# First stretch: v gathered on scaled tokens, k on tokens shifted in place, and the shift's part of v summed on VectorE

## The chip, the cores and the metric

The kernel runs on one core of one Trainium2 chip. The metric is the device time of one execution in microseconds (us). The core has TensorE (PE in the profile; PEld is its weight load), VectorE (DVE), ScalarE (ACT) and GpSimd (POOL), and SyncE (SP), whose queue issues nearly all loads; most stores to DRAM are issued from POOL's queue. A matmul accumulates in PSUM tiles; ScalarE or VectorE copies them out.

## The reference, cut to what matters

One inference step over 640 tokens (512 latent ones, 128 of context) and two layers. Both layers begin with a modulated norm; layer 0 is attention:

```python
sh, sc, ga = adaln(cond, w_mod[l], b_mod[l])     # silu(cond) @ w_mod + b_mod, in three
h = rms_norm(y, g_pre[l]) * (1.0 + sc) + sh       # 640 x 2048
q, k, v, g = split(h @ w_in_attn)                 # 2048, 512, 512 and 2048 columns
q = rms_norm(q, q_norm); k = rms_norm(k, k_norm)  # per head of 128, then rotary positions
o = blocked_attention(q, k, v)
y = y + ga * rms_norm((o * silu(g)) @ w_out, g_post[l])
```

Latent and context tokens have their own `cond`, hence their own shift and scale, one value per feature. Each product is made of three matmuls over operands split in a high and a low part (hi, lo; wh, wl). Layer 1 has a linear recurrence in place of attention; its code is the same in both kernels. k and v of the context tokens are also outputs (new_cache_k, new_cache_v).

## The kernel before, in words

The normalized tokens stand in five tiles `xn`, 128 tokens each. The first stretch (inside `tc.manual_schedule()`, so in the order written) goes over the 2048 features in eight passes of 256, and a ninth that only finishes. Pass n does this, with the pieces interleaved on TensorE:

- `gemv0` four times (kb = 0 to 3): 512 rows of w_mod, 256 columns of shift and 256 of scale in one tile `raw` of 1 MB, are multiplied with the conditions (`c32`, 32 columns of which two count). Four matmuls of 512 columns go to four groups of 32 rows of `pm`.
- `x_t`: eight transposes of token tiles; `row0` copies `pm` out, `cols0` turns the row into columns by eight small matmuls with `sel4`; three VectorE instructions then make scale and shift of this pass.
- `put`: hi = token x scale + shift on ScalarE, the same once more in full precision (`v`), lo = v - hi on VectorE; once for the latent and once for the context tokens, whose transposes come between.
- `load_wv`, `split_w`, `v_part`: 256 rows of v's weights are loaded and split, and one pass later, when hi and lo of these features stand, five token tiles are gathered into v: 30 matmuls of 128x512 per pass (2 feature blocks x 5 token tiles x 3). v's accumulators are three PSUM tiles `pg0` to `pg2`.

After it, v is copied out into two `qf` tiles (pool `pb`, two buffers for all uses of `qf`) and written to `v_s` and new_cache_v. Then come, by `gemm_nat`, one block of k and four blocks of q, each 240 matmuls over the finished hi and lo with weights loaded by 1-MB tiles and split into `wh`, `wl` (a ring of three). A block's three accumulators are `pd` tiles, of which there are four. `norm_rope` copies each accumulator to a `qf` tile, squares it into a `qs` tile (both on ScalarE), and makes norm and rotary positions on VectorE; POOL's queue writes the result to `k_s` or `q_s`. Eight blocks of g follow (`gemm_T`), and attention reads all from DRAM.

Beside the blocks runs a generator `gemv` (layer 1's modulation on VectorE, 32 steps of about four instructions of 128x1024). `background` is called once per 1-MB weight tile; it adds 32/36 to a credit and runs one step for each whole unit of it. Outside the manual stretch a scheduler sets the order on each engine; code that is written earlier has priority, and `split_w` above all.

Of the kernel before, what the change touches and what calls it, by code (L numbers as in the profile page):

```python
# [44 lines left out]
def hybrid_step(ctx: ExitStack, tc: tile.TileContext, i, o):  # L45
# [219 lines left out]

    def gemv0(fb, kb, pm):


        raw = rawp.tile([128, 2048], F32, name="raw", tag="raw")
        r4 = raw.rearrange("p (k a n) -> p k a n", k=4, a=2)  # L270
        for a in range(2):
            SY.dma_start(r4[:, :, a], i["w_mod"][0, kb * 512:kb * 512 + 512,
                                                 a * D + fb * 256:a * D + fb * 256 + 256]
                         .rearrange("(k p) n -> p k n", p=128))
        for j in range(4):
            PE.matmul(pm[32 * j:32 * j + 32], c32[:, kb * 4 + j], raw[:, j * 512:j * 512 + 512],  # L276
                      start=(kb == 0), stop=(kb == 3))

    def row0(pm):
        row = pa.tile([128, 512], F32, name="row", tag="row", bufs=1)  # L280
        S.copy(row, pm)
        return row

    def cols0(fb, pm, row):

        pc = pm[:, :8]
        for b in range(4):
            PE.matmul(pc[:, 2 * b:2 * b + 2], row[:, b * 128:b * 128 + 128], sel4, start=True, stop=True)
        kt = fb * 2
        tmp = small.tile([128, 2, 2, 2], F32, name="mt", tag="mt")  # L290
        bm = VA[:, 32:64].rearrange("p (a k) -> p a k", a=2)[:, :, kt:kt + 2]
        V.tensor_tensor(tmp, pc.rearrange("p (a f c) -> p a f c", a=2, f=2),
                        bm.unsqueeze(3).to_broadcast([128, 2, 2, 2]), op=add)
        V.scalar_tensor_tensor(scale[0][:, kt:kt + 2], tmp[:, 1], 1.0,
                               VA[:, kt:kt + 2].unsqueeze(2).to_broadcast([128, 2, 2]), op0=add, op1=mult)
        V.tensor_copy(shift[0][:, kt:kt + 2], tmp[:, 0])

    def put(k, c, src, t):
        sc, sh = scale[0][:, k, c:c + 1], shift[0][:, k, c:c + 1]
        n = t.stop - t.start  # L300
        v = pa.tile([128, NL], F32, name="v", tag="v", bufs=2)
# [9 lines left out]

    def load_wv(fb):
        w = pa.tile([128, 1024], F32, name="wv", tag="wv", bufs=2)
        SY.dma_start(w.rearrange("p (k n) -> p k n", k=2),
                     w_in[fb * 256:fb * 256 + 256, 2560:3072].rearrange("(k p) n -> p k n", p=128))
        return w

    def v_part(fb, k2, toks, w):

        k = fb * 2 + k2  # L320
        for m in toks:
            t = slice(TOFF[m], TOFF[m] + 128)
            b = slice(k2 * 512, k2 * 512 + 512)
            mm3(vacc[m // 2][:, m % 2], hi[:, k, t], lo[:, k, t], w[0][:, b], w[1][:, b], k == 0, k == KT - 1)

    VA = load_cols("VA", [fold2(i["g_pre"]), fold2(i["b_mod"])])
    with tc.manual_schedule():
        for m in range(5):
            SY.dma_start(xn[m], x_rows(m))
        for m in range(5):  # L330
            load_x(m)
        wv = None
        for n in range(9):
            now = n < 8
# [12 lines left out]
            if n:
                v_part(n - 1, 0, (4,), wv)
            if now:
                xt = [x_t(n * 2 + f) for f in range(2)]  # L350
                wn = split_w(wn)
                gemv0(n, 3, pm)
                row = row0(pm)
            if n:
                v_part(n - 1, 1, (0, 1), wv)
            if now:
                cols0(n, pm, row)
            if n:
                v_part(n - 1, 1, (2, 3, 4), wv)
            if now:  # L360
# [8 lines left out]
                wv = wn  # L369
    VB = load_cols("VB", [fold2(i["conv_w"][0]), fold(i["conv_b"][0])], 80)  # L370
# [50 lines left out]

    gv = gemv()
# [641 lines left out]
```

## Time and profile before

| what | value |
|---|---|
| time, median of 3 runs (lowest, highest) | 1950.09 us (1949.22, 1951.38) |
| the profiled execution | 1950.84 us, of which the span of the trace is 1949.1 us |
| PE busy | 1885.3 us, 97% of the span |
| PEld busy | 1675.4 us, 86% |
| DVE busy | 1324.5 us, 68% |
| ACT busy | 864.5 us, 44% |
| POOL busy | 136.2 us, 7% |
| read from and written to HBM | 273.03 MB, 29.43 MB |

Durations and starts come from the profiled execution, whose own time is the span and 1.7 us around it. It is 0.75 us above the median. A busy share is an average over stages with different limits; a line of the timeline gives the start, the duration, and in brackets the idle time before it and what released the instruction. A matmul's duration overlaps the next one's, so the cost of one is the difference of two starts. The DMA share is the mean over 16 engines and can pass 1.

### The profile page before, as it was taken

What the parts mean: (1) busy time and instruction counts of PE and PEld (TensorE: products, weight loads), DVE (VectorE), ACT (ScalarE), POOL (GpSimd) and SP (SyncE); (2) the same over time, 40 slices, a digit from 0 to 9 for tenths busy, and PEclk for the clock granted to TensorE, in tenths of its full rate; (3) what the DMA queues carried; (4) which work ended last, traced back from release to release, by engine and by line L of the source; (5) the groups of instructions that cost most, each with busy time, mean ns of one, the idle gap of its engine ahead of it and who ended that gap; (6) DMA issues with size and microseconds to landing.
All of it is one profiled execution on the core that took longest, in us unless ns stands there. A gap on an engine that the chain in (4) does not pass through costs nothing.

```text
span 1949.1 us, 26788 instructions
## 1 busy us (share of the span) xinstructions
PE 1885.3 (97%) x10857; PEld 1675.4 (86%) x10857; DVE 1324.5 (68%) x1856; ACT 864.5 (44%) x1256; POOL 136.2 (7%) x218
## 2 busy tenths in 40 slices
PE   4999999999999899999999999899999999999997
PEld 1567887879999899998888889899999999988886
DVE  3237859758365389998857775875775674798646
ACT  4441223222221288882223555666466456652222
POOL 0000000000000001110000000110110010020000
PEclk9999999999999999999999999999999999999999
DMA  9995435536454212225545674323322322537446
GB/s 341 348 321 195 162 123 184 178 119 198 157 175 150 86 38 74 74 74 198 180 155 187 234 260 130 122 72 96 120 95 92 101 79 86 175 110 253 146 136 220
DMA packets 195900, 304.20 MB, mean 156 GB/s; under 512 B 7344, under 2 KB 124720, under 8 KB 193856
## 3 DMA queue, kind: packets, MB, share of 16 engines
q1 hardware_dynamic: 188944, 274.10, 42.5%
q0 software_dynamic: 6832, 28.38, 4.0%
q8 instruction: 85, 1.39, 0.3%
q14 instruction: 39, 0.32, 0.0%
HBM read 273.03 MB, written 29.43 MB: 155 GB/s over the span
## 4 chain that ended last, share of the span: by engine, by line
PE 83%; DVE 6%; ACT 5%; issue 2%; DMA 2%; SPq 1%; POOL 0%; DVEq 0%; ACTq 0%; POOLq 0%
PE pd L184 22%; PE pd L185 22%; PE pd L186 22%; PE pd L215 2%; PE pd L217 2%; PE pd L218 2%; PE pm L276 2%; PE ph L631 1%; PE pg L184 1%; ACT L938 1%; PE pg L185 1%; PE pg L186 1%; PE sp L184 1%; PE sp L185 1%; PE sp L186 1%
## 5 line engine op out<-in xcount | busy, mean ns | idle before, releaser
L179 ACT CAST wh<-raw 128x1024 fp32r<-128x1024 f32 x248 | 258.1, 1048 | 606.1 <-PE pd L186 331.6
L180 DVE TENSOR_TENSOR wl<-raw,wh 128x1024 fp32r<-128x1024 f32 x248 | 301.6, 1222 | 238.9 <-ACT wh L179 238.1
L184 PE MATMUL pd<-wh,hi 128*128 128x512 f32 x1040 | 411.2, 396 | 3.6 <-ACT qf L498 2.5
L185 PE MATMUL pd<-wl,hi 128*128 128x512 f32 x1040 | 410.6, 395 | 0.0
L186 PE MATMUL pd<-wh,lo 128*128 128x512 f32 x1040 | 410.3, 394 | 0.0
L184 PE MATMUL pd<-hi,wh 128*128 128x322 f32 x1280 | 399.2, 312 | 0.0
L186 PE MATMUL pd<-hi,wl 128*128 128x322 f32 x1280 | 397.0, 310 | 1.1 <-DVE wl L180 1.1
L185 PE MATMUL pd<-lo,wh 128*128 128x322 f32 x1280 | 397.5, 311 | 0.0
L186 PEld LDWEIGHTS pd<-hi,wl 128*128 128x128 f32 x1280 | 241.5, 189 | 1.6 <-DVE wl L180 1.6
L185 PEld LDWEIGHTS pd<-lo,wh 128*128 128x128 f32 x1280 | 242.2, 189 | 0.1
L184 PEld LDWEIGHTS pd<-hi,wh 128*128 128x128 f32 x1280 | 241.4, 189 | 0.5 <-ACT wh L179 0.3
L184 PEld LDWEIGHTS pd<-wh,hi 128*128 128x128 f32 x1040 | 195.8, 188 | 50.7 <-ACT qf L498 2.9
L186 PEld LDWEIGHTS pd<-wh,lo 128*128 128x128 f32 x1040 | 195.9, 188 | 46.1
L185 PEld LDWEIGHTS pd<-wl,hi 128*128 128x128 f32 x1040 | 195.9, 188 | 45.5 <-DVE wl L180 0.3
L741 DVE SCALAR_TENSOR_TENSOR ga<-raw,cT,ga 128x512 f32<-128x512 f32 x256 | 175.8, 748 | 15.7 <-DMA ga<-b_mod 13.0
L395 DVE SCALAR_TENSOR_TENSOR ga<-raw,cT,ga 128x1024 f32<-128x1024 f32 x120 | 149.8, 1279 | 27.4 <-DMA raw<-w_mod 26.8
L184 PE MATMUL pd<-xh,wh 128*128 128x322 f32 x256 | 81.5, 320 | 5.2 <-ACT xh L876 4.4
L215 PE MATMUL pd<-hi,wh 128*128 128x256 f32 (+1 forms) x256 | 80.7, 315 | 6.0 <-ACT wh L179 4.3
L218 PE MATMUL pd<-hi,wl 128*128 128x256 f32 (+1 forms) x256 | 80.2, 313 | 0.0
L217 PE MATMUL pd<-lo,wh 128*128 128x256 f32 (+1 forms) x256 | 80.1, 313 | 0.0
L185 PE MATMUL pd<-xl,wh 128*128 128x322 f32 x256 | 80.1, 314 | 0.0
L186 PE MATMUL pd<-xh,wl 128*128 128x322 f32 x256 | 79.9, 313 | 0.0
(238 smaller groups left out, 2813.6 us busy)
## 6 DMA issues: line engine op xcount, KB each, us to landing
raw<-w_mod SPq DMA_DIRECT2D x64, 1024.0 KB
raw<-w_in_lru SPq DMA_DIRECT2D x40, 1024.0 KB
raw<-w_in_attn SPq DMA_DIRECT2D x36, 1024.0 KB
raw<-w_mod SPq DMA_DIRECT2D x64, 512.0 KB
raw<-w_out_attn SPq DMA_DIRECT2D x20, 1024.0 KB
raw<-w_out_lru SPq DMA_DIRECT2D x20, 1024.0 KB
g_s<-qf POOLq DMA_DIRECT2D x16, 322.0 KB, 3.4
raw<-g_s SPq DMA_DIRECT2D x16, 322.0 KB
```

The costliest lines, as they stand in the source:

```text
L179: S.copy(wh, src)
L180: V.tensor_tensor(wl, src, wh.bitcast(F32), op=sub)
L184: PE.matmul(out, ah, bh, start=first, stop=False)
L185: PE.matmul(out, ah, bl, start=False, stop=False)
L186: PE.matmul(out, al, bh, start=False, stop=last)
L215: PE.matmul(outs[f], wh[:, c], hi[:, k, t], start=(k == 0 and first[f]), stop=False, skip_group_check=True)
L217: PE.matmul(outs[f], wh[:, c], lo[:, k, t], start=False, stop=False, skip_group_check=True)
L218: PE.matmul(outs[f], wl[:, c], hi[:, k, t], start=False, stop=(k == KT - 1), skip_group_check=True)
L276: PE.matmul(pm[32 * j:32 * j + 32], c32[:, kb * 4 + j], raw[:, j * 512:j * 512 + 512], start=(kb == 0), stop=(kb == 3))
L395: V.scalar_tensor_tensor(acc[c], w2[:, k2], cT[:, k, c:c + 1], acc[c], op0=mult, op1=add)
L631: PE.transpose(pt[:, c * 128:c * 128 + 128], P[:, b, c * 128:c * 128 + 128], ident)
L741: V.scalar_tensor_tensor(acc[:, c], raw[:, k4 * 512:k4 * 512 + 512], cT[:, kb * 4 + k4, c:c + 1], acc[:, c], op0=mult, op1=add)
```

## The change: what it does

The first stretch now has 17 passes. Passes 0 to 7 read only the scale half of w_mod. One `raw` tile holds 1024 rows of 256 columns, for two `gemv0`, each of four matmuls of 256 columns. `put` makes hi and lo from the token times the scale alone (lo by one VectorE instruction), and v is gathered on these. Passes 8 to 15 read the shift half, and `add_shift` adds the shift to hi and lo in place: u = hi + lo, hi = u + shift, lo = u + shift - hi. Behind it, in passes 9 to 16, k is gathered on the finished tokens in the way v was. v and k are copied into `xn` tiles, which are free by then, and written to the scratch arrays `v_r` and `k_r`. The `gemm_nat` block of k is gone; `norm_rope` loads k from `k_r`.

What v lacks is shift @ w_v, one row of 512 for each condition. The generator `v_shift` makes it first thing in the background: it loads v's weights again (four tiles of 1 MB), sums shift x weight over the 16 feature blocks on VectorE (32 instructions of 128x512, two conditions), splits the sum, adds over the partitions by four matmuls with `ones` into a `pd` tile, loads v back from `v_r` into `qf` tiles, adds, and writes v_s and new_cache_v. Then it goes on with `gemv`. The credit per call is 40/32.

```diff
+    def gemv0(part, fb, kb, pm):
+        if kb % 2 == 0:
+            raw = rawp.tile([128, 2048], F32, name="raw", tag="raw")
+            SY.dma_start(raw.rearrange("p (k n) -> p k n", k=8),
+                         i["w_mod"][0, kb * 512:kb * 512 + 1024, part * D + fb * 256:part * D + fb * 256 + 256]
                          .rearrange("(k p) n -> p k n", p=128))
+            rawg[0] = raw
         for j in range(4):
-            PE.matmul(pm[32 * j:32 * j + 32], c32[:, kb * 4 + j], raw[:, j * 512:j * 512 + 512],
+            n = ((kb % 2) * 4 + j) * 256
+            PE.matmul(pm[32 * j:32 * j + 32, :256], c32[:, kb * 4 + j], rawg[0][:, n:n + 256],
                       start=(kb == 0), stop=(kb == 3))
...
-        S.activation(hi[:, k, t], src, AF.Identity, scale=sc, bias=sh)
-        S.activation(v[:, :n], src, AF.Identity, scale=sc, bias=sh)
-        V.tensor_tensor(lo[:, k, t], v[:, :n], hi[:, k, t].bitcast(F32), op=sub)
+        S.activation(hi[:, k, t], src, AF.Identity, scale=sc)
+        V.scalar_tensor_tensor(lo[:, k, t], src, sc, hi[:, k, t].bitcast(F32), op0=mult, op1=sub)
+
+    def add_shift(k):
+        u = pa.tile([128, TE], F32, name="u", tag="u", bufs=2)
+        V.tensor_tensor(u, hi[:, k, :TE].bitcast(F32), lo[:, k, :TE].bitcast(F32), op=add)
+        for c, t in ((0, slice(0, NL)), (1, slice(PO, TE))):
+            sh = shift[0][:, k, c:c + 1]
+            S.activation(hi[:, k, t], u[:, t], AF.Identity, bias=sh)
+            V.scalar_tensor_tensor(lo[:, k, t], u[:, t], sh, hi[:, k, t].bitcast(F32), op0=add, op1=sub)
...
+    def evac(acc, dst):
+        for j, (a, ms) in enumerate(zip(acc, PAIRS)):
+            n = len(ms)
+            f = xn[j][:, :n * 512].rearrange("p (m n) -> p m n", n=512)
+            (V.tensor_copy if j == 1 else S.copy)(f, a)
+            G.dma_start(dst[ms[0] * 128:ms[0] * 128 + n * 128].rearrange("(m p) n -> p m n", p=128), f)
...
-        for n in range(9):
-            now = n < 8
+        for n in range(17):
+            now = n < 16
+            part, fb, pb_ = int(n < 8), n % 8, (n - 1) % 8
...
+            elif now:
+                if n == 8:
+                    evac(acc, v_r)
+                    acc = accs()
+                for f in range(2):
+                    add_shift(fb * 2 + f)
+            else:
+                evac(acc, k_r)
...
+    def v_shift():
+        acc = pb.tile([128, 1024], F32, name="ga0", tag="ga0")
+        a2 = acc.rearrange("p (c n) -> p c n", c=2)
+        for kb in range(4):
+            w = load_w(w_in, kb * 512, 4, 2560, 512)
...
+                        V.scalar_tensor_tensor(a2[:, c], wk, sh, a2[:, c], op0=mult, op1=add)
+                if k4 % 2:
+                    yield
+        pg = psd()
+        ah, al = split_w(acc)
+        for c in range(2):
+            PE.matmul(pg[:, c], ones, ah[:, c * 512:c * 512 + 512], start=True, stop=False)
+            PE.matmul(pg[:, c], ones, al[:, c * 512:c * 512 + 512], start=False, stop=True)
+        for ms in PAIRS:
...
+            vf = pb.tile([128, 2, 512], F32, name="qf", tag="qf", bufs=2)
+            SY.dma_start(vf[:, :n], v_r[rows].rearrange("(m p) n -> p m n", p=128))
+            V.tensor_tensor(vf[:, :n], vf[:, :n], pg[:, ms[0] // 4].unsqueeze(1).to_broadcast([128, n, 512]), op=add)
+            G.dma_start(v_s[rows].rearrange("(m p) n -> p m n", p=128), vf[:, :n])
...
-        credit[0] += 32 / 36
+        credit[0] += 40 / 32
...
-    norm_rope(gemm_nat(w_in, 2048, background), "k", k_s, o["new_cache_k"])
+    norm_rope([None] * 3, "k", k_s, o["new_cache_k"])
```

How instructions move is shown at three places; a row gives the line, the operation, what it writes and reads, and its size, and the numbers behind names tell tiles of one name apart. The first is one pass on VectorE, before:

```order
L180 TENSOR_TENSOR wl_792<-wv_750,wh_791 128x1024
L292 TENSOR_TENSOR mt_814<-pm_742,VA_173 128x8
L294 SCALAR_TENSOR_TENSOR scale0_152<-mt_814,VA_173 128x4
L296 COPY shift0_150<-mt_814 128x4
L304 TENSOR_TENSOR lo_119<-v_827,hi_118 128x512
L304 TENSOR_TENSOR lo_119<-v_831,hi_118 128x512
L304 TENSOR_TENSOR lo_119<-v_838,hi_118 128x128
L304 TENSOR_TENSOR lo_119<-v_842,hi_118 128x128
```

and now, in the last of the shift passes, which has no instruction for the scale and none on fresh tokens, but sums and shifts in place:

```order
L182 TENSOR_TENSOR wl_1676<-raw_1673,wh_1675 128x1024
L299 TENSOR_TENSOR shift0_152<-pm_1431,VA_172 128x4
L314 TENSOR_TENSOR u_1493<-hi_120,lo_121 128x642
L318 SCALAR_TENSOR_TENSOR lo_121<-u_1493,shift0_152,hi_120 128x512
L318 SCALAR_TENSOR_TENSOR lo_121<-u_1493,shift0_152,hi_120 128x128
L314 TENSOR_TENSOR u_1499<-hi_120,lo_121 128x642
L182 TENSOR_TENSOR wl_1710<-raw_1673,wh_1709 128x1024
L318 SCALAR_TENSOR_TENSOR lo_121<-u_1499,shift0_152,hi_120 128x512
L318 SCALAR_TENSOR_TENSOR lo_121<-u_1499,shift0_152,hi_120 128x128
```

The split of the weight tile for the first q block (`wl_1710`) stands between the two feature blocks there. The second place is TensorE where the second q block (q1) ends and the third (q2) begins; `pd` are their accumulators. Before, q2 follows q1 directly:

```order
L184 MATMUL pd_1906<-wh_2195,hi_118 128x512
L185 MATMUL pd_1906<-wl_2196,hi_118 128x512
L186 MATMUL pd_1906<-wh_2195,lo_119 128x512
L184 MATMUL pd_2306<-wh_2311,hi_118 128x512
L185 MATMUL pd_2306<-wl_2312,hi_118 128x512
L186 MATMUL pd_2306<-wh_2311,lo_119 128x512
```

Now the four matmuls with `ones`, written into the tile `pd_2348`, come between:

```order
L186 MATMUL pd_2053<-wh_2314,hi_120 128x512
L187 MATMUL pd_2053<-wl_2315,hi_120 128x512
L188 MATMUL pd_2053<-wh_2314,lo_121 128x512
L473 MATMUL pd_2348<-wh_2349,ones_131 128x512
L474 MATMUL pd_2348<-wl_2350,ones_131 128x512
L473 MATMUL pd_2348<-wh_2349,ones_131 128x512
L474 MATMUL pd_2348<-wl_2350,ones_131 128x512
L186 MATMUL pd_2455<-wh_2460,hi_120 128x512
L187 MATMUL pd_2455<-wl_2461,hi_120 128x512
```

The third place is ScalarE at the same point, where CAST makes the weights' high part and COPY and ACTIVATE on a `pd` tile are those of `norm_rope`. Before:

```order
L179 CAST wh_2161<-raw_2159 128x1024
L179 CAST wh_2195<-raw_2159 128x1024
L179 CAST wh_2311<-raw_2309 128x1024
L406 COPY row_2140<-pd_2123 2x1024
L179 CAST wh_2345<-raw_2309 128x1024
L459 COPY qf_2235<-pd_1904 128x1024
L460 ACTIVATE qs_2236<-pd_1904 128x1024
L459 COPY qf_2261<-pd_1905 128x1024
```

and now, where `ga0_1743` is v_shift's sum, and the copy of q1's first tile goes into `qf_2384`, the buffer that v_shift's second add used:

```order
L181 CAST wh_2314<-raw_2278 128x1024
L181 CAST wh_2349<-ga0_1743 128x1024
L181 CAST wh_2460<-raw_2458 128x1024
L181 CAST wh_2494<-raw_2458 128x1024
L181 CAST wh_2536<-raw_2534 128x1024
L527 COPY qf_2384<-pd_2051 128x1024
L528 ACTIVATE qs_2385<-pd_2051 128x1024
L158 ACTIVATE ra_2392<-rv_2390 128x8
L527 COPY qf_2410<-pd_2052 128x1024
L528 ACTIVATE qs_2411<-pd_2052 128x1024
```

On VectorE the first two adds of v_shift stand there right behind `wl_2537`, the split that belongs to `wh_2536`, and the third one behind five multiply-adds of the modulation; on POOL's queue v_shift's writes stand between the last one of q0 and the first one of q1.

## Rows read from the trace of the kernel before

**Rows 1.** Waits of the first 160 us: TensorE's and those of the loads' queue (SPq). Columns: who waited, for whom, us in all, times, the longest in us.
```profile
PE pm L276 <- DMA raw<-w_mod: 20.0, 3, 16.5
...
SPq L272 <- PE pm L276: 43.4, 24, 4.9
```
**Rows 2.** Busy time by windows (start:end in us; length; busy us and count of each engine; PEclk, the granted clock as a share of full speed; DMA share; GB/s): the start, pass 1, pass 2, pass 7, pass 8 (gathers alone), and 3 us of the k block.
```profile
20.90:37.30 16.40, 10.00 (x50) 3.48 (x50) 6.23 (x17) 5.48 (x9) 0.00 (x0) 0.92 1.09 352
37.30:53.50 16.20, 15.91 (x81) 8.81 (x80) 3.37 (x9) 5.46 (x11) 0.00 (x0) 0.87 1.10 352
53.58:67.40 13.82, 13.82 (x84) 8.00 (x88) 3.60 (x9) 5.70 (x11) 0.00 (x0) 1.00 1.10 352
...
122.73:136.50 13.77, 13.77 (x81) 8.09 (x82) 3.54 (x9) 5.64 (x11) 0.00 (x0) 1.00 0.94 314
136.50:143.41 6.91, 6.91 (x31) 5.41 (x30) 4.35 (x7) 5.21 (x9) 0.56 (x1) 1.00 0.72 235
...
151.00:154.00 3.00, 3.00 (x9) 2.33 (x8) 2.96 (x9) 0.50 (x2) 0.38 (x1) 0.50 0.53 181
```
**Rows 3.** One pass on TensorE, from its first gemv0 (L276) to that of the next pass; L309 and L365 are transposes, L288 the matmuls of cols0, pg the gathers. Columns: start, us, engine, line, operation, count.
```profile
95.01 1.07 PE L276 MATMUL pm<-raw,c 128*32 128x512 f32 x8
95.01 0.16 PEld L276 LDWEIGHTS pm<-raw,c 128*32 128x32 f32 x8 [0.17 <-issue]
96.01 0.50 PE L184 MATMUL pg<-wh,hi 128*128 128x512 f32 x1
...
101.97 1.04 PE L309 MATMUL p<-ident,xn 128*128 128x128 f32 x8
102.94 1.07 PE L276 MATMUL pm<-raw,c 128*32 128x512 f32 x8
...
105.44 0.95 PE L288 MATMUL pm<-sel,row 128*128 128x2 f32 x8
106.25 0.48 PE L184 MATMUL pg<-wh,hi 128*128 128x512 f32 x1
...
108.47 0.44 PE L365 MATMUL p<-ident,xn 128*128 128x128 f32 x2
108.84 0.64 PE L276 MATMUL pm<-raw,c 128*32 128x512 f32 x4
```
**Rows 4.** Busy time by windows in the q blocks, columns as in rows 2: the first block, the third, and the sum over all four.
```profile
204.60:260.30 55.70, 55.70 (x242) 45.14 (x241) 35.60 (x56) 15.22 (x20) 2.56 (x4) 1.00 0.48 164
...
316.00:371.70 55.70, 55.70 (x242) 45.15 (x241) 46.22 (x65) 13.82 (x18) 2.00 (x3) 1.00 0.56 193
...
sum 222.90, PE 222.90 PEld 179.46 DVE 159.10 ACT 57.80 POOL 8.58; mean PE 55.73 PEld 44.86 DVE 39.78 ACT 14.45 POOL 2.15
```
**Rows 5.** The start on TensorE: the second gemv0 of pass 0 and the way to pass 1. Columns as in rows 3.
```profile
25.36 1.94 PE L276 MATMUL pm<-raw,c 128*32 128x512 f32 x8 [2.43 <-DMA raw<-w_mod]
...
30.24 1.62 PE L309 MATMUL p<-ident,xn 128*128 128x128 f32 x8
31.79 1.07 PE L276 MATMUL pm<-raw,c 128*32 128x512 f32 x8
...
37.32 1.08 PE L276 MATMUL pm<-raw,c 128*32 128x512 f32 x4
```
**Rows 6.** From the columns of the modulation to hi and lo in one pass (timeline of VectorE and ScalarE). Columns as in rows 3.
```profile
106.49 0.17 DVE L292 TENSOR_TENSOR mt<-pm,VA 128x8 f32<-128x8 f32 x1 [6.98 <-PE pm L288]
106.97 0.78 ACT L302 ACTIVATE hi<-p,shift,scale 128x512 fp32r<-128x512 f32 x1 [2.31 <-DVE shift L296]
108.45 0.69 DVE L304 TENSOR_TENSOR lo<-v,hi 128x512 fp32r<-128x512 f32 x1 [1.51 <-ACT v L303]
```
**Rows 7.** From v to k, all engines' timeline. Columns as in rows 3.
```profile
142.85 0.88 POOL L499 DMA_DIRECT2D v_s<-qf  x1 [130.88 <-ACT qf L498]
142.91 1.22 DVE L498 COPY qf<-pg 128x1024 f32<-128x1024 f32 x1 [1.27 <-PE pg L186]
...
144.54 0.50 PE L184 MATMUL pd<-wh,hi 128*128 128x512 f32 x1 [0.78 <-DVE VC L106]
...
149.38 0.58 ACT L498 COPY qf<-pg 128x512 f32<-128x512 f32 x1 [4.73 <-DMA v_s<-qf]
...
150.02 0.50 PE L184 MATMUL pd<-wh,hi 128*128 128x512 f32 x1 [2.47 <-ACT qf L498]
```
**Rows 8.** Durations by line, operation and shape over the whole span: count, us in all, mean ns of one, idle time before them and its releasers.
```profile
L179 ACT CAST wh<-raw 128x1024 fp32r<-128x1024 f32 x248 | 258.1, 1048 | 606.1 <-PE pd L186 331.6 <-PE pd L185 177.0 <-issue 25.9
L180 DVE TENSOR_TENSOR wl<-raw,wh 128x1024 fp32r<-128x1024 f32 x248 | 301.6, 1222 | 238.9 <-ACT wh L179 238.1
L741 DVE SCALAR_TENSOR_TENSOR ga<-raw,cT,ga 128x512 f32<-128x512 f32 x256 | 175.8, 748 | 15.7 <-DMA ga<-b_mod 13.0 <-DMA raw<-w_mod 2.5
L978 DVE TENSOR_TENSOR lo<-raw,hi 128x642 fp32r<-128x642 f32 x16 | 12.8, 825 | 1.0 <-ACT hi L977 0.8
L459 ACT COPY qf<-pd 128x1024 f32<-128x1024 f32 x10 | 10.2, 1015 | 12.8 <-PE pd L186 12.8
L460 ACT ACTIVATE qs<-pd 128x1024 f32<-128x1024 f32 x10 | 10.3, 1028 | 0.0
```
**Rows 9.** DMA issues on POOL's queue: what is written, count, size of one, median us from issue to landing.
```profile
q_s<-qs POOLq DMA_DIRECT2D x8, 512.0 KB, 3.8
...
k_s<-qs POOLq DMA_DIRECT2D x2, 512.0 KB, 4.4
```

More of the change, by code (lines that the diff above doesn't have):

```diff
@@ L264, in load_x @@
         V.tensor_scalar(xn[m], xn[m], rx, None, op0=mult)
[L266 to L273, printed above, removed]
+    rawg = {}
+    def gemv0(part, fb, kb, pm):
[3 more added lines that the diff above has]
+                         i["w_mod"][0, kb * 512:kb * 512 + 1024, part * D + fb * 256:part * D + fb * 256 + 256]
@@ L281, in row0, with cols0 @@
-        S.copy(row, pm)
-        return row
-    def cols0(fb, pm, row):
-        pc = pm[:, :8]
-        for b in range(4):
+        row = pa.tile([128, 256], F32, name="row", tag="row", bufs=1)
+        S.copy(row, pm[:, :256])
+        return row
+    def cols0(part, fb, pm, row):
+        pc = pm[:, 256:260]
+        for b in range(2):
             PE.matmul(pc[:, 2 * b:2 * b + 2], row[:, b * 128:b * 128 + 128], sel4, start=True, stop=True)
         kt = fb * 2
[L290 to L296, printed above, removed]
@@ L298, in put @@
-    def put(k, c, src, t):
-        sc, sh = scale[0][:, k, c:c + 1], shift[0][:, k, c:c + 1]
-        n = t.stop - t.start
-        v = pa.tile([128, NL], F32, name="v", tag="v", bufs=2)
-        S.activation(hi[:, k, t], src, AF.Identity, scale=sc, bias=sh)
-        S.activation(v[:, :n], src, AF.Identity, scale=sc, bias=sh)
-        V.tensor_tensor(lo[:, k, t], v[:, :n], hi[:, k, t].bitcast(F32), op=sub)
+        bm = VA[:, 32 + part * 16 + kt:34 + part * 16 + kt].unsqueeze(2).to_broadcast([128, 2, 2])
@@ new lines, in cols0 @@
+        pc = pc.rearrange("p (f c) -> p f c", f=2)
+        if part == 0:
+            V.tensor_tensor(shift[0][:, kt:kt + 2], pc, bm, op=add)
+        else:
+            tmp = small.tile([128, 2, 2], F32, name="mt", tag="mt")
+            V.tensor_tensor(tmp, pc, bm, op=add)
+            V.scalar_tensor_tensor(scale[0][:, kt:kt + 2], tmp, 1.0,
+                                   VA[:, kt:kt + 2].unsqueeze(2).to_broadcast([128, 2, 2]), op0=add, op1=mult)
+    def put(k, c, src, t):
+        sc = scale[0][:, k, c:c + 1]
+        S.activation(hi[:, k, t], src, AF.Identity, scale=sc)
+        V.scalar_tensor_tensor(lo[:, k, t], src, sc, hi[:, k, t].bitcast(F32), op0=mult, op1=sub)
@@ L331, in hybrid_step @@
             load_x(m)
-        wv = None
-        for n in range(9):
-            now = n < 8
+        wv, acc = None, accs()
+        for n in range(17):
+            now = n < 16
+            part, fb, pb_ = int(n < 8), n % 8, (n - 1) % 8
             if now:
                 pm = ps.tile([128, 512], F32, name="pm", tag="pm", bufs=1)
-                gemv0(n, 0, pm)
-                wn = load_wv(n)
+                gemv0(part, fb, 0, pm)
+                wn = load_wv(fb, 2560 if n < 8 else 2048)
             if n:
-                v_part(n - 1, 0, (0, 1), wv)
+                gather(acc, pb_, 0, (0, 1), wv)
             if now:
-                gemv0(n, 1, pm)
+                gemv0(part, fb, 1, pm)
             if n:
-                v_part(n - 1, 0, (2, 3), wv)
+                gather(acc, pb_, 0, (2, 3), wv)
             if now:
-                gemv0(n, 2, pm)
+                gemv0(part, fb, 2, pm)
             if n:
-                v_part(n - 1, 0, (4,), wv)
+                gather(acc, pb_, 0, (4,), wv)
             if now:
-                xt = [x_t(n * 2 + f) for f in range(2)]
+                if n < 8:
+                    xt = [x_t(n * 2 + f) for f in range(2)]
                 wn = split_w(wn)
-                gemv0(n, 3, pm)
+                gemv0(part, fb, 3, pm)
                 row = row0(pm)
             if n:
-                v_part(n - 1, 1, (0, 1), wv)
+                gather(acc, pb_, 1, (0, 1), wv)
             if now:
-                cols0(n, pm, row)
+                cols0(part, fb, pm, row)
             if n:
-                v_part(n - 1, 1, (2, 3, 4), wv)
-            if now:
+                gather(acc, pb_, 1, (2, 3, 4), wv)
+            if n < 8:
                 for f in range(2):
@@ L458, in norm_rope @@
             qs = pb.tile([128, 2, 512], F32, name="qs", tag="qs", bufs=2)
-            S.copy(qf[:, :n], a[:, :n])
+            if a is None:
+                SY.dma_start(qf[:, :n], k_r[ms[0] * 128:ms[0] * 128 + n * 128].rearrange("(m p) n -> p m n", p=128))
+                a = qf
+            else:
+                S.copy(qf[:, :n], a[:, :n])
             S.activation(qs[:, :n], a[:, :n], AF.Square)
```

38 lines of the change are left out of this document (23 added, 15 removed).

## The prediction, made before the changed kernel ran

> **What bounds the kernel now.** I read the time shares first, then the waits, then the first 430 us in windows and row by row, because every edit lies there; from the attention on both kernels issue the same work. By the table above TensorE is busy for 97% of the span. In the first stretch the reader should see three things. (a) The transfers don't set the pace: the stretch runs at a DMA share of 1.09 to 1.10 [rows 2], yet TensorE waits for w_mod only three times, 20.0 us in all and 16.5 of it once, whereas it is the DMA queue that waits 43.4 us, 24 times, for TensorE to free a tile [rows 1]. (b) A pass takes 13.82 us at share 1.10 and 13.77 at 0.94 [rows 2]: its length follows TensorE's work. (c) Therefore a change is worth what it adds to or takes from TensorE's own line, plus new waits.
>
> **A pass, taken apart** [rows 3]. From 95.01 to 108.84: 13.83 us. One gemv0 (four matmuls of 512 columns) takes 96.01 - 95.01 = 1.00; take 0.995, four make 3.98. Token transposes 102.94 - 101.97 = 0.97; cols0 106.25 - 105.44 = 0.81; prompt transposes 108.84 - 108.47 = 0.37. The rest, 7.70, is 30 gathering matmuls, 0.257 each. The same matmul inside a gemm block costs 55.7 / 240 = 0.232 [rows 4].
>
> **The changed passes.** A gemv0 of 256 columns has no row. It can't be under half, 0.50, if its columns count alone, and not over 1.00; with 0.16 us of weight load kept [rows 3] and the rest halved it is 0.16 + 0.835/2 = 0.58, which I take.
> - Passes 1 to 7 (scale half): 13.83 - 4 x 0.415 - 0.40 for half the cols0 matmuls = 11.77.
> - Passes 8 to 15 (shift half, no transposes): 7.70 + 0.41 + 4 x 0.58 = 10.43.
> - Pass 16, gathers alone: as the last one before, 6.91 [rows 2].
> The start: four w_mod tiles are waited for before; now two hold the whole first pass. The second one let TensorE go on at 25.36 [rows 5]. After it come two gemv0 (2.0 at the low clock), transposes 1.55 (31.79 - 30.24), and the way from the end of the fourth gemv0 (32.8) to pass 1 (37.32), 4.5 us, which loses about 1 since put has one ScalarE instruction less per piece: 25.36 + 2.0 + 1.55 + 3.5 = 32.4. Pass 1 keeps its clock loss: its window shows 0.87 and 16.2 us, 2.4 over the others [rows 2].
>
> Does the in-place shift stall TensorE? After cols0, VectorE makes the shift (0.17) and u (0.83, the 642-column subtraction stands for it), ScalarE hi (0.78), VectorE lo (0.69, as put's): 2.5 us [rows 6, 8]. TensorE has nine gathers and the next gemv0 meanwhile, 2.3 + 0.58 = 2.9. So nothing, with 0.4 us to spare; were the cover gone, 0.8 x 7. At the one seam where v turns into k, VectorE's 1.22-us evacuation [rows 7] and the constant loads come ahead of u: 2 us, once.
>
> New q0 start: 32.4 + (11.77 + 2.4) + 6 x 11.77 + (10.43 + 2.0) + 7 x 10.43 + 6.91 + 0.5 for the hand-over = 209.5. Before it is 204.6, where the window of the first q block begins [rows 4]. The first part is **+5**. In that figure the old boundary is gone for good: there TensorE waited 0.78 and 2.47 us, the latter for the ScalarE copy that waited 4.73 us for a v_s write out of a qf tile [rows 7], and afterwards ran at half clock from 151 to 154 [rows 2], where half of 3 us is 1.5 lost. The accumulators now go to three separate tiles that nobody else wants.
>
> **The q blocks.** v_shift puts into them 32 VectorE steps of 512 columns, 0.75 each = 24 [rows 8], beside four loads (4 MB; the DMA share there is 0.48 to 0.56, room enough [rows 4]) and four matmuls with ones, 0.93. The new price is a wait at the seam q1 to q2. These matmuls write the fourth accumulator tile, the only free one, right behind q1's last matmul (time 0). q2's first matmul then needs q1's first tile, which the ScalarE copy into a qf tile and the square after it free. But both qf tiles are held by v_shift's first two adds until their v_s writes have landed; the copy waits for the second. The chain, with durations of [rows 8]: the ring frees a weight tile at 0, wh 1.05, wh 2.1, wl 3.3 (the adds stand behind it on VectorE), add 4.5, add 5.7, then the write on POOL's queue. How long until it has landed is bounded by rows of 512-KB writes: 3.8 (q_s), 4.4 (k_s) [rows 9] and 6.5 (149.38 after 142.85, the one that was waited for) [rows 7]. I take 5.2, between the last two: 10.9. Copy 1.0, square 1.0 [rows 8]: 12.9, less the 0.93 covered: **12** of waiting, 10.6 by the shortest row, 13.3 by the longest. While ScalarE stands in that copy, wh of q2's later chunks and the next squares queue behind it; nothing else on TensorE could run. Then the third add waits for its load into the first qf tile, its writes must land, and q1's second tile is copied late: 0 to 4.7, I take 2. After 2.5 us of idling the granted clock stood at 0.50 for 3 us [rows 2]; after a longer wait I take 2 (1.5 to 3.4). Sum at the seam: 0.9 + 12 + 2 + 2 = **+17**.
>
> The Trainium skill, "DMA: Bandwidth & Descriptors", section "Anatomy of one DMA — SWDGE (gpsimd) path", gives about 2.0 us fixed plus bytes over 436 GB/s for a transfer on this queue; for 512 KB that makes an estimate of 3.2 us. The rows here, 3.8 to 6.5, are all longer; by the page's figure the wait would be 10 and the total some 2 us lower.
>
> **The sum.** +5 + 17 = +22 on the profiled run: span 1949.1 to 1971, and with the 1.7 us around it 1973; that run lies 0.75 above the median shown, so **1972** against 1950.1.
>
> **Rivals.**
> 1. *VectorE falls behind in the q blocks.* Now 159 us of 223 [rows 4]. Then 24 for the steps, 3 for the adds, 1 for a split, and I allow 5 for table setup that stands later now: some 192, or 86%; with uneven placement the fullest block, 46.2 of 55.7 now, could pass 55. A late wl would cost 10 us over two blocks: 1982. For it: the written order puts up to five multiply-adds of the modulation between two wl. Against: the mean stays under the span, and the ring is three deep.
> 2. *The wait at the seam is hidden or short* (the writes land early, or q2's first tile was freed otherwise): only the first part and a little remain, 1950 + 5 + 1 + 2 = 1958. Against it: the same pattern shows at 149.38 [rows 7].
> 3. *Not slower: the narrow gemv0 costs only its weight loads.* Place: the 60 gemv0 of passes 1 to 15. If it takes 0.16 instead of 0.58, that returns 60 x 0.42 = 25 and the end is 1947. It decides from 0.21 us on (22 / 60 = 0.37 less). Against: its four matmuls of 512 columns take 0.995, and one gather of 512 columns 0.257 [rows 3], so columns set the time.
> 4. *Dearer passes:* gemv0 keeps its 1.00, 60 x 0.42 = 25 more, 1997; or lo is late in seven shift passes, +5.6, 1978.
> The change does do what it says: v is gathered on scaled tokens in passes 1 to 8, k in 9 to 16.
>
> A rule that speaks to the clock term: "TensorE: Matmul & The Clock Gate", section "HAM oscillation — how this bites in real kernels" of the Trainium skill, says that idle gaps put the clock back to half, so that the next work starts cold. The 0.50 at 151 to 154 behind the 2.47-us wait [rows 2] agrees; it makes the seam dearer than its idle time.
>
> **How the numbers follow.** Main case, first part and seam both as worked out, 0.64, its own range 1964 to 1981 (seam 11 to 20, first part 3 to 11). VectorE behind 0.15, 1981 to 1992. Wait hidden 0.11, 1953 to 1960. Not slower 0.06, 1945 to 1954. Dear gemv0 0.04. The range 1956 to 1988 leaves out rival 3, the lower part of 2, the upper part of 1 and the dear gemv0, near 2 in 10. A measurement of this kernel tells 0.2% from no change: 1946.2 to 1954.0. Faster takes most of rival 3: 0.04; same the rest of it and the edge of rival 2: 0.06; slower 0.90.
>
> **What would show it.** The windows of passes 2 to 7 at 11.8 us and of passes 9 to 15 at 10.4, with gemv0 at 0.58 apart; q0 starting near 209.5; no wait for a qf copy near the first hand-over; one TensorE wait of about 12 us on ScalarE's qf copy between q1 and q2, ScalarE's own wait on the v_s write, clock 0.50 behind it; VectorE near 86% in the q blocks; the attention unchanged but later. Wrong would be: repeated waits of TensorE on wl in the q blocks (rival 1), no long wait at the seam (rival 2), or passes far from those lengths (3, 4).

## The result, and the profile after

The changed kernel takes 1970.04 us (median of 4 runs, 1969.17 to 1970.84) against 1950.64 us for the one before (4 runs, 1949.22 to 1951.38): ratio 1.0103, 95% interval 1.009 to 1.0116. It is slower by about 20 us, against 22 forecast, and the spans of the two profiled executions differ by 20.0 us. The first lines of the page of the profile after:

```profile
span 1969.1 us, 27426 instructions
...
PE 1895.8 (96%) x11117; PEld 1678.9 (85%) x11117; DVE 1378.5 (70%) x1941; ACT 864.5 (44%) x1264; POOL 140.5 (7%) x224
```

TensorE is busy 10.5 us longer and the span is 20 us longer, so about half of the loss is busy time of TensorE (matmuls at half clock count in it) and half is idle time. The waits say where the idle time is (columns: who waited, for whom, us in all, times, longest); the window is the first 460 us:

```profile
PE pm L282 <- DMA raw<-w_mod: 18.8, 2, 16.5
PE pd L186 <- ACT qs L528: 12.7, 1, 12.7
...
PE pg L186 <- ACT hi L317: 1.2, 1, 1.2
```

One line is new and large, the second: one wait of 12.7 us for a square of `norm_rope`. The last line is the seam where v turns into k. The wait of 2.5 us for a qf copy that stood at the old boundary [rows 7] is not in the list any more.

Now the first stretch by windows, as [rows 2]: the start, pass 1, pass 6, pass 8, one shift pass, the last gathers, and the first six microseconds behind the long wait.

```profile
20.90:33.44 12.54, 7.54 (x47) 3.89 (x47) 6.93 (x17) 4.44 (x7) 0.00 (x0) 1.00 1.09 353
33.44:47.08 13.64, 13.47 (x77) 8.37 (x76) 3.49 (x7) 3.31 (x6) 0.00 (x0) 1.00 1.01 333
93.90:105.58 11.68, 11.68 (x77) 7.53 (x76) 3.66 (x8) 3.31 (x6) 0.00 (x0) 1.00 0.68 224
117.27:127.73 10.46, 10.46 (x67) 6.39 (x67) 2.85 (x6) 3.06 (x5) 0.88 (x1) 1.00 0.70 234
182.05:192.50 10.45, 10.45 (x67) 6.39 (x66) 4.91 (x9) 3.34 (x6) 0.00 (x0) 1.00 0.72 235
202.89:210.03 7.14, 7.14 (x32) 5.55 (x30) 4.07 (x7) 3.10 (x5) 0.57 (x1) 1.00 0.52 179
335.08:341.00 5.92, 5.92 (x14) 4.71 (x15) 5.69 (x11) 1.62 (x3) 1.12 (x2) 0.50 0.68 229
```

TensorE is busy in the whole of each regular pass, at DMA shares of 0.68 to 0.72 in these rows, so here the transfers are far from setting the pace. The first q block begins at 210.03; before it began at 204.60 [rows 4]: +5.4. Rows of one scale pass, as [rows 3], give the new price of gemv0 by the difference of two starts, 106.15 - 105.58 = 0.57 us (the first row and the gather after it):

```profile
105.58 0.64 PE L282 MATMUL pm<-raw,c 128*32 128x256 f32 x8
106.15 0.50 PE L186 MATMUL pg<-wh,hi 128*128 128x512 f32 x1
...
107.74 0.64 PE L282 MATMUL pm<-raw,c 128*32 128x256 f32 x8
```

Between 106.15 and 107.74 lie six gathers: 1.59 us, 0.265 each, while six in a q block take 1.39. Last the seam of the second and third q block, by the timeline of all engines (start, us, engine, line, operation; in brackets the idle time before and what ended it):

```profile
321.30 0.40 PE L473 MATMUL pd<-wh,ones 128*128 128x512 f32 x1
321.50 1.99 ACT L181 CAST wh<-raw 128x1024 fp32r<-128x1024 f32 x2 [5.90 <-PE pd L188]
...
324.13 2.35 DVE L182 TENSOR_TENSOR wl<-raw,wh 128x1024 fp32r<-128x1024 f32 x2
326.40 2.35 DVE L480 TENSOR_TENSOR qf<-qf,pd 128x1024 f32<-128x1024 f32 x2
327.91 0.71 POOL L481 DMA_DIRECT2D v_s<-qf  x1 [34.66 <-DVE qf L480]
329.05 0.73 POOL L481 DMA_DIRECT2D v_s<-qf  x1 [0.43 <-DVE qf L480]
333.09 1.01 ACT L527 COPY qf<-pd 128x1024 f32<-128x1024 f32 x1 [9.61 <-DMA v_s<-qf]
334.00 1.03 ACT L528 ACTIVATE qs<-pd 128x1024 f32<-128x1024 f32 x1
335.08 0.80 PE L186 MATMUL pd<-wh,hi 128*128 128x512 f32 x1 [12.70 <-ACT qs L528]
335.14 0.69 DVE L480 TENSOR_TENSOR qf<-qf,pd 128x512 f32<-128x512 f32 x1 [0.41 <-DMA qf<-v_r]
...
340.80 0.51 PE L187 MATMUL pd<-wl,hi 128*128 128x512 f32 x1
```

This is read upwards from the matmul at 335.08. TensorE waits for a square, which follows a copy; ScalarE stood 9.61 us in front of that copy until the second v_s write had landed; the write left POOL's queue at 329.05, behind the second add on VectorE; the adds came behind two splits. The matmul at 335.08 takes 0.80 us and not 0.40: the granted clock is 0.50 until 341, as the last window above shows (the last row is where it ends).

The balance: +5.4 at the start of the q blocks; at the seam 335.08 - 321.30 = 13.8, of which 12.7 is waiting and the rest the ones matmuls; and 2.8 for the clock, as the run with tiles of their own shows below. That is 22.0. One of the modulation's matmul groups with `sel` stood in front of the g blocks before and stands inside them now; such a group takes 1.85 us, the distance of its first and the next matmul in these rows of before:

```profile
430.03 0.62 PE L403 MATMUL pd<-wh,sel 128*2 128x512 f32 x2
...
431.88 0.32 PE L184 MATMUL pd<-hi,wh 128*128 128x322 f32 x1
```

Where the g blocks begin the difference is therefore 20.1 us (their first matmul starts at 452.01 against 431.88), and at the end it is 20.0: the group comes back in the g blocks, and later stages return about as much. One place of this is the attention, where the clock is near half for some 7 us before (first row) and some 4 us after (second):

```profile
676.00:683.00 7.00, 5.77 (x21) 5.68 (x22) 4.15 (x7) 4.87 (x10) 2.09 (x1) 0.53 0.22 66
```

```profile
699.00:703.00 4.00, 4.00 (x19) 3.90 (x18) 3.13 (x6) 2.62 (x7) 0.66 (x1) 0.57 0.40 115
```

### The profile page after: what moved, and what is told of

Read it like the earlier page. It is cut to its first block, busy times and chain, and to the rows that moved or that the text cites. A ratio compares the mean times of both kernels' runs of the same rounds, so it can differ in the third digit from the quotient of the medians.

```text
span 1969.1 us, 27426 instructions
## 1 busy us (share of the span) xinstructions
PE 1895.8 (96%) x11117; PEld 1678.9 (85%) x11117; DVE 1378.5 (70%) x1941; ACT 864.5 (44%) x1264; POOL 140.5 (7%) x224
## 4 chain that ended last, share of the span: by engine, by line
PE 78%; DVE 7%; ACT 5%; issue 5%; DMA 3%; SPq 1%; POOL 0%; DVEq 0%; ACTq 0%; POOLq 0%
PE pd L186 19%; PE pd L187 19%; PE pd L188 19%; PE pg L186 2%; PE pg L188 2%; PE pm L282 2%; PE pg L187 2%; PE pd L217 2%; PE pd L219 2%; PE pd L220 2%; PE ph L692 1%; DVE wl L182 1%; ACT L999 1%; PE ph L186 1%; PE sp L188 1%
## 5 line engine op out<-in xcount | busy, mean ns | idle before, releaser
L181 ACT CAST wh<-raw 128x1024 fp32r<-128x1024 f32 x240 | 249.8, 1048 | 548.7 <-PE pd L188 293.7
L182 DVE TENSOR_TENSOR wl<-raw,wh 128x1024 fp32r<-128x1024 f32 x240 | 291.8, 1222 | 203.1 <-ACT wh L181 202.1
L186 PE MATMUL pd<-wh,hi 128*128 128x512 f32 x960 | 380.0, 396 | 13.8 <-ACT qs L528 12.7
L187 PE MATMUL pd<-wl,hi 128*128 128x512 f32 x960 | 379.4, 395 | 0.0
L188 PE MATMUL pd<-wh,lo 128*128 128x512 f32 x960 | 379.2, 395 | 0.0
L186 PEld LDWEIGHTS pd<-wh,hi 128*128 128x128 f32 x960 | 181.1, 189 | 57.3 <-ACT qs L528 13.1
L188 PEld LDWEIGHTS pd<-wh,lo 128*128 128x128 f32 x960 | 181.1, 189 | 42.6
L187 PEld LDWEIGHTS pd<-wl,hi 128*128 128x128 f32 x960 | 181.1, 189 | 42.2 <-DVE wl L182 0.3
L802 DVE SCALAR_TENSOR_TENSOR ga<-raw,cT,ga 128x512 f32<-128x512 f32 x256 | 175.7, 746 | 15.1 <-DMA ga<-b_mod 12.8
```

The lines of the kernel that those rows point to most:

```text
L181: S.copy(wh, src)
L182: V.tensor_tensor(wl, src, wh.bitcast(F32), op=sub)
L802: V.scalar_tensor_tensor(acc[:, c], raw[:, k4 * 512:k4 * 512 + 512], cT[:, kb * 4 + k4, c:c + 1], acc[:, c], op0=mult, op1=add)
```

## The experiments

**Tiles of their own for v_shift.** Three tiles for its loads and adds, in place of the two shared ones:

```diff
-            vf = pb.tile([128, 2, 512], F32, name="qf", tag="qf", bufs=2)
+            vf = pb.tile([128, 2, 512], F32, name="vf", tag="vf", bufs=3)
```

> The changed kernel, with three tiles of their own for v_shift's loads and adds, in place of the two qf tiles that norm_rope also uses. Theory (the 12.7-us wait of TensorE at the seam of the second and third q block comes from the shared qf tiles alone): q1's first accumulator is copied and squared before q1 ends, the wait falls to under 1 us, the half clock behind it goes too (6 us at half, 3 lost), and the time is 1970 - 12.7 - 3 = 1954, 1953 to 1956. Rival A (the seam also pays for the accumulator tile that the ones matmuls take, so that q2 waits for a copy and a square in any case): a wait of about 3 us stays, 1958 to 1960. Rival B (VectorE is late in the q blocks and its adds and splits set the seam): the wait moves to a wl split and over half of it stays, 1962 or more.

Measured: 1954.9 us (10 runs) beside 1949.7 for the kernel before (26 runs), ratio 1.0029 (1.0019 to 1.0038). The wait for the square is gone; the waits of TensorE in the q blocks hold one entry, 0.7 us. The timeline of the same seam:

```profile
316.23 1.02 ACT L527 COPY qf<-pd 128x1024 f32<-128x1024 f32 x1 [1.71 <-PE pd L188]
317.14 1.03 ACT L528 ACTIVATE qs<-pd 128x1024 f32<-128x1024 f32 x1
...
320.22 0.40 PE L473 MATMUL pd<-wh,ones 128*128 128x512 f32 x1
...
321.14 0.40 PE L186 MATMUL pd<-wh,hi 128*128 128x512 f32 x1
...
324.11 0.39 PE L187 MATMUL pd<-wl,hi 128*128 128x512 f32 x1
...
325.31 2.94 DVE L480 TENSOR_TENSOR vf<-vf,pd 128x1024 f32<-128x1024 f32 x3
...
328.40 0.48 PE L186 MATMUL pd<-wh,hi 128*128 128x512 f32 x1 [0.71 <-DVE rr L159]
```

q1's first accumulator is copied and squared at 316 to 318, before the ones matmuls; in the changed kernel that happened at 333 to 335. The adds come as late behind the ones matmuls as before (325.31 - 320.22 = 5.1 us, as 326.40 - 321.30), and q2's start doesn't wait for them. This execution is 1.1 us ahead already at the ones matmuls (320.22 against 321.30). q2's first matmul starts at 321.14 and not at 335.08, 13.9 us earlier, so the seam gives 12.9; the matmul that starts at 340.80 in the changed kernel, where the half clock ends, is q2's fourteenth and starts at 324.11 here, which is another 2.8. So the shared tiles made the long wait, and rival B (VectorE) falls. Of rival A (the accumulator tile) at most the 0.7 us is left, where 3 were expected: that wait ends right behind the third add, which reads the tile of the ones matmuls (325.31 + 2.94 = 328.25). That TensorE waits there for this tile is likely, but not shown.

**Without the shift's part of v.** v_shift's loads, VectorE steps, ones matmuls and adds are left out:

```diff
-                    evac(acc, v_r)
+                    evac(acc, v_s)
...
     def v_shift():
-        acc = pb.tile([128, 1024], F32, name="ga0", tag="ga0")
...
+        for _ in range(8):
+            yield
         yield from gemv()
```

> The changed kernel without the shift's part of v: v goes from its accumulators to v_s and new_cache_v directly, and v_shift's loads, its 32 VectorE steps, the four ones matmuls and the adds are left out (the modulation steps keep their places). Theory: what is left against the kernel before is the first part alone, 5.4 us; time 1950.6 + 5.4 - up to 2 = 1954 to 1956, and no more than 1 us under the run with tiles of its own for v_shift. Rival B (VectorE's added load costs time beside the q blocks): 3 us or more under that run.

Measured: 1952.59 us (11 runs) beside 1949.7, ratio 1.0018 (1.0008 to 1.0028), 1.4 below the range expected. It lies 2.3 us under the run with own tiles, more than the 1 us expected and under the 3 us of the rival. The ones matmuls (0.9) and the 0.7-us wait, which is gone here, make 1.6 of it; in the traces the way from the first q block to the first g block is 1.8 us shorter (209.72 to 435.09 here, 208.97 to 436.14 there). The rest is within the scatter of these runs. Against the kernel before, 2.9 us remain. Its first q block begins at 209.72, against 204.60 before [rows 4], 5.1 later, and its span is only 2.2 longer (1951.3 against 1949.1). (The window from 316.00 in [rows 4] is not quite the third block before: a group with `sel` lies ahead of it, and the block begins near 318.7.) The later stages return the rest, and the clock is near half for a shorter time there. Two places of it, here:

```profile
681.00:686.00 5.00, 4.13 (x16) 4.09 (x17) 2.86 (x5) 3.45 (x7) 2.09 (x1) 0.66 0.29 84
...
1268.00:1273.00 5.00, 4.15 (x17) 4.16 (x18) 2.12 (x5) 3.00 (x4) 0.14 (x2) 0.66 0.05 17
```

and in the kernel before, where the first place is the row from 676 shown above and the second this one:

```profile
1263.00:1271.00 8.00, 5.19 (x21) 5.19 (x22) 4.09 (x7) 3.68 (x6) 0.14 (x2) 0.57 0.29 102
```

That the clock alone returns it is argued from these rows, not shown by a run.

**The sums made twice**, with own tiles:

```diff
+                    if k == 0:
+                        V.tensor_scalar(d2[:, c], wk, sh, None, op0=mult)
+                    else:
+                        V.scalar_tensor_tensor(d2[:, c], wk, sh, d2[:, c], op0=mult, op1=add)
                     if k == 0:
                         V.tensor_scalar(a2[:, c], wk, sh, None, op0=mult)
```

> The changed kernel with v_shift's own tiles, and with its 32 VectorE steps done twice (the second sum is thrown away): 24 us more of VectorE beside the first two q blocks. Theory (the steps fill idle time and the splits keep their place): within 1.5 us of the run with own tiles, 1954.9. Rival (VectorE is so full that its work sets the q blocks): waits of TensorE on wl of 5 us or more in the q blocks, 1960 or more.

Measured: 1955.39 us (9 runs) beside 1950.71, ratio 1.0022 (1.001 to 1.0034); with own tiles alone it was 1.0029. Windows of the two first q blocks (columns as in rows 2):

```profile
210.00:266.00 56.00, 56.00 (x243) 45.42 (x242) 53.08 (x106) 16.78 (x20) 3.94 (x7) 1.00 0.62 210
266.00:321.00 55.00, 55.00 (x239) 44.56 (x238) 54.79 (x86) 13.37 (x18) 2.02 (x3) 1.00 0.45 158
```

The two blocks hold 107.9 us of VectorE's work, 19 more than in the changed kernel (88.8) and not 24, since steps of the modulation move back. VectorE is busy for 54.79 of 55.00 us in the second block, and TensorE for all 55.00. TensorE's list of waits has no entry in the q blocks, not even the 0.7 us. So even a full VectorE didn't hold up the splits, which keep their places among the background's steps (they are written with high priority). The load of the sums on VectorE costs nothing here.

**The kernel before with the free tiles.** v goes from its accumulators to three token tiles, and nothing else is changed:

```diff
+            if not now:
+                for j, (a, ms) in enumerate(zip(vacc, PAIRS)):
+                    nn = len(ms)
+                    f = xn[j][:, :nn * 512].rearrange("p (m n) -> p m n", n=512)
+                    (V.tensor_copy if j == 1 else S.copy)(f, a)
+                    G.dma_start(v_s[ms[0] * 128:ms[0] * 128 + nn * 128].rearrange("(m p) n -> p m n", p=128), f)
...
-    for a, ms in zip(vacc, PAIRS):
-        n = len(ms)
-        vf = pb.tile([128, 2, 512], F32, name="qf", tag="qf", bufs=2)
```

> The kernel before with one part of the change alone: v is copied out of its accumulators into three of the token tiles, which are free by then, and written to v_s and new_cache_v from these. Theory: the 2.47-us wait of the k block for a copy into a qf tile goes, and the half clock behind it (1.5 us lost): 1950.6 - 4 = 1946.6, 1945.5 to 1948. Rival (the wait only moves, since the memory of the token tiles is taken over by the next pool, whose first writers then wait for the v_s writes): within 1 us of 1950.6.

Measured: 1949.04 us (11 runs) beside 1949.7, ratio 0.9989 (0.9978 to 1.0). The expected 4 us don't show in the time. In the trace they do at their place: this execution was 1.0 us behind the one of before when the k block began (145.59 against 144.54), and where the g blocks begin it is 3.2 us ahead (430.48 against 433.73 below), which is 4.2 us. It gives a part back where nothing was changed. At the beginning of the g blocks both kernels wait 1.1 us for a wl; the two rows below are that wait here and the stretch behind it, and the two after them the same of the kernel before:

```profile
430.48 0.41 PE L186 MATMUL pd<-hi,wl 128*128 128x322 f32 x1 [1.10 <-DVE wl L180]
...
433.00:436.00 3.00, 3.00 (x14) 3.00 (x13) 3.00 (x8) 0.17 (x1) 0.00 (x0) 0.56 0.88 318
```

```profile
433.73 0.41 PE L186 MATMUL pd<-hi,wl 128*128 128x322 f32 x1 [1.10 <-DVE wl L180]
...
433.00:437.00 4.00, 3.27 (x25) 3.06 (x26) 4.00 (x7) 1.81 (x4) 0.00 (x0) 1.00 0.99 296
```

Behind the same wait, and the same narrow matmuls around it, the clock falls to 0.56 here and stays at 1.00 before; the lead shrinks from 3.2 to 1.8 us. The later stages take another half microsecond. So the term was sized rightly at its place, and what later stages grant decides whether it can be seen in the end. Why the clock fell there in one kernel and not in the other stays open.

**The gemv0 together in the shift passes.** All four at the start of passes 8 to 15:

```diff
                 gemv0(part, fb, 0, pm)
+                if n >= 8:
+                    for kb in range(1, 4):
+                        gemv0(part, fb, kb, pm)
...
-            if now:
+            if n < 8:
                 gemv0(part, fb, 1, pm)
```

> The changed kernel with the four gemv0 of a shift pass issued one after the other at the pass's start, so that the gathers of passes 8 to 15 are interrupted by them once and not four times. Theory (each switch from gemv0 to a gather costs about 0.2 us: 6 gathers behind one take 1.59 us, at the q blocks' rate they would take 1.39): 3 x 0.2 x 8 = 4.8 less, 1965, 1964 to 1967; the passes take 9.8 in place of 10.4. Rival (gathers are slower here because of the loads beside them): the passes stay at 10.4, 1969 to 1971. Rival (the two w_mod tiles come too late when wanted at once): TensorE waits for w_mod, 1971 or more.

Measured: 1961.26 us (5 runs) beside 1949.7, ratio 1.0058 (1.0045 to 1.0072), 8.8 under the changed kernel where 4.8 were expected. One pass of it on TensorE:

```profile
155.61 1.93 PE L282 MATMUL pm<-raw,c 128*32 128x256 f32 x32
157.47 0.51 PE L186 MATMUL pg<-wh,hi 128*128 128x512 f32 x1
...
165.11 1.93 PE L282 MATMUL pm<-raw,c 128*32 128x256 f32 x32
166.97 0.50 PE L186 MATMUL pg<-wh,hi 128*128 128x512 f32 x1
```

The pass takes 165.11 - 155.61 = 9.50 us in place of 10.46. Four gemv0 together take 157.47 - 155.61 = 1.86, where four apart took 4 x 0.57 = 2.28, and the gathers lose less too. A switch costs 0.96 / 3 = 0.32 us: 0.14 in the gemv0 and 0.18 in the gathers between two of them. The same transfers run beside the gathers, so it isn't these that slow them. Eight passes give 7.7 of the 8.8 us. Another 1.2 is TensorE's wait for `hi` where v turns into k, which is not in the list of waits any more. The wait at the seam is still there, 12.8 us.

**Both together**: own tiles, and the four gemv0 together in every pass, so in the scale passes too.

```diff
-                gemv0(part, fb, 0, pm)
+                for kb in range(4):
+                    gemv0(part, fb, kb, pm)
                 wn = load_wv(fb, 2560 if n < 8 else 2048)
...
-            vf = pb.tile([128, 2, 512], F32, name="qf", tag="qf", bufs=2)
+            vf = pb.tile([128, 2, 512], F32, name="vf", tag="vf", bufs=3)
```

> The changed kernel with v_shift's own tiles, and with the four gemv0 together at the start of every pass, the scale passes too. Theory (both costs are independent, and a switch between gemv0 and gather costs about 0.3 us, as the shift passes with gemv0 together gave 0.96 us each for three switches): 1954.9 - 8.8 for the shift passes - 7 x 0.9 for the scale passes = 1940, 1937 to 1943, faster than both kernels. Rival (in the scale passes the two w_mod tiles come too late when all four gemv0 want them first): TensorE waits for w_mod in passes 1 to 7 and the time stays at 1945 to 1948.

Measured: 1936.77 us (5 runs, 1934.21 to 1938.13) beside 1950.71, ratio 0.9927 (0.9914 to 0.9939): faster than both kernels, and 3 us under the expectation, just outside its range. Its waits on w_mod, and the third scale pass:

```profile
PE pm L282 <- DMA raw<-w_mod: 16.9, 2, 15.9
```

```profile
42.92:53.68 10.76, 10.76 (x78) 7.98 (x77) 3.66 (x8) 3.21 (x6) 0.00 (x0) 1.00 1.07 350
```

A scale pass takes 10.76 us in place of 11.68, which is 0.31 for each of three switches again, and TensorE waits for w_mod only at the start; but the DMA share is at 1.07 and 350 GB/s there, so early on little is left; two passes later it is at 0.78.

**The kernel before with the gemv0 together**, the same edit on the wide gemv0:

> The kernel before with the four gemv0 of a pass together at its start, nothing else. A pass then wants four w_mod tiles (4.2 MB) at once. Theory that TensorE's line sets the pass before: it loses three switches, 0.9 us in each of seven passes, 1950 - 6 = 1944. Rival that the transfers stand right behind it (a pass moves 4.7 MB; at the 352 GB/s of the first stretch that is 13.4 us against 13.8): the passes only come down to 13.4 and TensorE waits for w_mod in each: 1947, or above 1950 when the four tiles are freed too late to be loaded again in time.

Measured: 1952.28 us (11 runs) beside 1950.71, ratio 1.001 (1.0 to 1.0021): no gain. The waits of TensorE in its first 460 us, and three gemv0 in a row:

```profile
PE pm L276 <- DMA raw<-w_mod: 25.3, 11, 16.2
...
PE pd L184 <- ACT qf L494: 3.6, 1, 3.6
...
94.73 2.78 PE L276 MATMUL pm<-raw,c 128*32 128x512 f32 x24
```

It waits for w_mod 11 times and not 3 [rows 1], and the old boundary costs 3.6 instead of 2.5. A pass that wants four 1-MB tiles at once runs into the transfers. The half-width passes, which want two, could be put together without such waits.

## Why the prediction was right

The forecast of 1972 us with a range of 1956 to 1988 held the 1970.0 us, and the mechanism was the one named: two costs, one of TensorE's own work and one a wait.

- **The pass.** gemv0 was taken as 0.58 and takes 0.57; scale passes 11.77 forecast, 11.68 measured; shift passes 10.43 and 10.45; the stall where v turns into k 2.0, measured 12.39 - 10.46 = 1.9 (pass 9 runs from 127.73 to 140.12). The last gathers took 7.14 against 6.91 (the window of [rows 2] for them begins 0.18 us behind their start). Rivals 3 and 4 fall with these rows.
- **The price of gemv0** is right by luck in its second term. The 0.58 was 0.42 for half the columns and 0.16 of weight load. In a row of four a narrow gemv0 adds (1.93 - 0.64) / 3 = 0.43 us (the rows of the run with the gemv0 together). Three wide ones in a row take 2.78 (the row of the kernel before with the gemv0 together) and one alone 1.07 [rows 3], so a wide one adds (2.78 - 1.07) / 2 = 0.86, just twice as much with as many weight loads. The 0.57 - 0.43 = 0.14 that does not shrink with the columns is what a switch costs the gemv0, and no run shows a share of the weight load in it.
- **The start.** Pass 1 was put at 32.4 and began at 33.44: gemv0, transposes and the small chain took 1 us longer; in return pass 1 lost 2.0 us to the later ones (13.64 - 11.68) and not 2.4. The terms of the first part add up to 210.0 and not to the 209.5 that is written, so they give +5.4, and +5.4 was measured (210.03).
- **The price inside a pass.** The working let the gathers be 0.257 and named no reason. The runs with the gemv0 together show it: a shift pass has four switches of 0.32 us, 1.3 us of the 3.5 by which its 10.45 are over 30 matmuls at the rate of the q blocks (6.96).
- **In-place shift.** No wait inside the regular shift passes, as forecast: the 0.4 us to spare was enough.
- **The seam.** 12 forecast, 12.7 measured; the chain was the right one, but the closeness is in part luck, since two errors nearly cancel. VectorE came later than worked out: its splits began at 324.13, 2.8 us after the time 0 of 321.30 (2.1 forecast), and two splits stood ahead of the adds, not one, so the second write left at 329.05, 7.75 us after time 0 instead of 5.7. The write in turn landed after 4.0 us (333.09 - 329.05) and not 5.2. The third add cost nothing where 2 was taken; the clock cost 2.8 where 2 was taken, inside its bounds of 1.5 to 3.4. So first part and seam came to 22.0 as forecast, and the total lies 2 us lower because later stages, which the forecast left unchanged, returned 2.
- **The Trainium skill's figure** ("DMA: Bandwidth & Descriptors", section "Anatomy of one DMA — SWDGE (gpsimd) path") made an estimate of 3.2 us for such a write. Here 4.0 was measured, nearer to that estimate than to the 5.2 taken, and still above it.
- **The old boundary.** Its wait is gone in the changed kernel, as forecast, and the run with the free tiles alone shows 4.2 us for wait and clock in the trace at their place.
- **Rival 1**, VectorE behind, had 0.15. VectorE's load was forecast nearly right (48.92, 39.88, 42.92 and 56.36 us in the four blocks, 188 in all against 192), but the conclusion that a block above 55 would hold TensorE up was wrong: the fourth has 56.36 of 58.44 and no wait of TensorE, and the run with the sums made twice had 54.79 of 55.00 and lost nothing.
- **Rival 2**, the wait hidden, is what own tiles make of the kernel: 1958 worked out for it, 1954.9 measured.

The windows of the four q blocks, from which the shares of VectorE are read (the third holds the half clock, the fourth a group with `sel`):

```profile
210.03:265.70 55.67, 55.67 (x242) 45.16 (x241) 48.92 (x99) 16.18 (x19) 3.99 (x7) 1.00 0.60 201
265.70:321.30 55.60, 55.60 (x242) 45.05 (x240) 39.88 (x60) 10.80 (x14) 2.02 (x3) 1.00 0.50 174
335.08:393.57 58.49, 58.49 (x240) 47.28 (x241) 42.92 (x64) 14.16 (x19) 3.14 (x5) 0.95 0.57 188
393.57:452.01 58.44, 58.44 (x257) 46.16 (x256) 56.36 (x75) 16.68 (x21) 2.01 (x3) 1.00 0.54 185
```

## What to carry to other kernels

A tile tag that two producers share is a queue: before giving background work a buffer of the foreground, follow the buffer to the moment its last reader, often a DMA write, has landed, and ask who is next in line for it. Count a change of matmul kind on TensorE as work of its own (0.32 us each here), and put the small ones together as long as the loads they want can be there at once. Before counting a background step's engine time as a loss, see whether it can get ahead of the work that is waited for: here, with the splits written at high priority, VectorE could be filled to the brim.

## What the runs showed that was not expected

- Six gathers behind a gemv0 took 1.59 us, six in a q block 1.39, and four gemv0 in a row 1.86 against 2.28 apart: the loss lies at the change from one kind to the other on both sides.
- VectorE at 54.79 of 55.00 us busy cost no TensorE time.
- Behind one and the same wait of 1.1 us the granted clock fell to 0.56 in one kernel and stayed at 1.00 in another whose work there is the same, so that a gain of some microseconds made early was partly gone at the end; differences under some 2 us between these kernels say little about an edit unless the trace shows them at their place.
